# The first weight pieces of a mixer: split by ScalarE and VectorE into spare weight buffers, in a written order

## The chip, the cores and the metric

The kernel runs on one core of a Trainium2 chip, as one program. The metric is the device time of one launch in microseconds, the median of three runs. Engines are named as the profile names them: PE is TensorE, DVE VectorE, ACT ScalarE, POOL GpSimd, SP SyncE; PEld is PE's weight load.

## The reference, cut to what matters

Two layers run over 256 tokens of width 1024, in float32. Each layer has a mixer and a mixture of experts:

```
h = rms_norm(x) * (1 + scale_m(c)) + shift_m(c)
z = h @ w_in                       # 1024 x 7680, in one product
m = sum_i sigmoid(gate_i) * (attention_i(z) @ w_proj_i)      # i = A, B, C
x = x + gate_m(c) * (m @ w_out)
h = rms_norm(x) * (1 + scale_f(c)) + shift_f(c)
x = x + gate_f(c) * HierMoE(h)     # one group of four, two experts of eight in it
```

scale, shift and gate come from c by a product with ada_w. The change touches the beginning of `h @ w_in` in both layers.

## The kernel before

**The product with w_in.** It runs in 15 chunks of 512 columns, and a chunk in four pieces of 256 rows of w_in (128x1024 elements in SBUF). PE works in a float32 type of reduced precision, so every operand is kept as a high and a low part: for a piece of weights w, `whi` is a rounded copy (ACT, a CAST) and `wlo = w - whi` (DVE). The activations are treated the same way, as `hi` and `lo`, eight k-blocks of each. Three products are added up, hi·whi, hi·wlo and lo·whi, which makes 24 matmuls of 128x256 columns for a piece. `whi` and `wlo` come from the pool `wk` with two buffers each (tags w4a, w4b), so the CAST of a piece has to wait until PE has done all matmuls of the piece two before it. Pieces are called c0p0 to c0p3 for chunk 0, c1p0 to c1p3 for chunk 1, and so on.

**The beginning of a mixer.** `raw_t` transposes x into xT; the last of its four copies out of PSUM (`self.rest`, L272) is held back and issued by `modulated`. `modulated` works out rstd by some small instructions on DVE (L256, L233 to L242), PE spreads it over the partitions as R, and then, for each k, DVE multiplies xT by scale and R (L292), ACT adds the shift and writes hi (L294), and DVE writes lo (L289). In layer 0 scale and shift are finished only shortly before (L190, L195, L214). Ahead of that, the two pieces c0p0 and c0p1 are split: the CAST on ACT (L327), the subtraction on POOL (L330). c0p2 and c0p3 are split by `gemm` when the pool's two buffers come free, with the subtraction on DVE.

**Behind each chunk.** Where a chunk holds queries or keys, ACT copies four shifted strips out of PSUM (L484, four copies of 32x512), DVE multiplies by cosine and sine (L485, L486), and POOL adds (L487). In between DVE works on the next step's ada_w product (L175, with a first step on ACT, L173), which is needed much later.

**Order.** A scheduler with a timeline of its own orders the instructions of each engine. Only what `keep_in_program_order` names keeps its written order. Loads go over SP's queue into pairs of a pool of ten (`slot`, 2 MB for a pair); a load is issued when its pair is free.

The lines of the kernel after the change are a little shifted: split L327, L330 become L333, L334; L292, L289, L294 become L296, L290, L298; L484 to L487 become L487 to L490.

Of the kernel before, what the change touches and what calls it, by code (L numbers as in the profile page):

```python
# [10 lines left out]
F32 = mybir.dt.float32  # L11
F32R = mybir.dt.float32r
# [9 lines left out]
P = 128  # L22
SEQ = 256
D = 1024
KD = D // P
# [28 lines left out]
def bc(ap, at, n):  # L54

    a = [list(e) for e in ap.ap]
    a.insert(at, [0, n])
    return bass.AP(tensor=ap.tensor, offset=ap.offset, ap=a)


class Kernel:
# [197 lines left out]
    def raw_t(self, c):  # L259

        nc = self.nc
        p = self.acc()
        for kk in range(2):
            k = 2 * c + kk
            for t in range(2):
                nc.tensor.transpose(p[:, kk * 256 + t * P:kk * 256 + (t + 1) * P],
                                    self.x[:, t, k * P:(k + 1) * P], self.ident)
        to, p = self.xT[:, 2 * c:2 * c + 2, :], p.rearrange("p (k n) -> p k n", k=2)
        if c < 3:
            nc.scalar.copy(to, p)  # L270
        else:
            self.rest = lambda: self.tc.keep_in_program_order(nc.vector.tensor_copy(to, p))  # L272

    def hilo(self):
        return (self.wk.tile([P, KD, 256], F32R, name=nm, tag=tag) for nm, tag in (("hi", "w8a"), ("lo", "w8b")))

    def modulated(self, l):

        nc, xT = self.nc, self.xT
        hi, lo = self.hilo()  # L280
        scale, shift = self.mcol[l][:, 1, :], self.mcol[l][:, 0, :]
        r = self.rstd()
        self.rest()
        R = self.acc()[:, :256]
        for t in range(2):
            self.mm(R[:, t * P:(t + 1) * P], bc(r[:, t], 1, P), self.ident, t == 0, t == 1, skip_group_check=True)

        def low(k):
            nc.vector.scalar_tensor_tensor(lo[:, k, :], xT[:, k, :], shift[:, k:k + 1], hi[:, k, :].bitcast(F32),  # L289
                                           op0=OP.add, op1=OP.subtract)  # L290
        for k in range(KD):
            i = nc.vector.scalar_tensor_tensor(xT[:, k, :], xT[:, k, :], scale[:, k:k + 1], R,  # L292
                                               op0=OP.mult, op1=OP.mult)
            nc.scalar.activation(hi[:, k, :], xT[:, k, :], AF.Identity, bias=shift[:, k:k + 1])  # L294
            if k > 1:
                self.tc.keep_in_program_order(i)  # L296
            if k:
                low(k - 1)  # L298
        low(KD - 1)
        return hi, lo  # L300

    def to_hilo(self, src, done):

# [15 lines left out]
            two(k, p.rearrange("p (a n) -> p a n", a=2))  # L319
        return hi, lo  # L320

    def split(self, w, early=False):

        nc, n = self.nc, w.shape[1]
        whi, wlo = (self.wk.tile([P, n, 1024 // n], F32R, name=f"{nm}{n}", tag=tag, bufs=2)
                    for nm, tag in (("whi", "w4a"), ("wlo", "w4b")))
        c = nc.scalar.copy(whi, w)  # L327
        if early:
            self.tc.keep_in_program_order(c)
        (nc.gpsimd if early else nc.vector).tensor_sub(wlo, w, whi.bitcast(F32))  # L330
        return whi, wlo

    def gemm(self, pieces, hi, lo, prods):  # L333
# [44 lines left out]
    def mixer(self, l, fill):  # L378

        nc, tc, io = self.nc, self.tc, self.io  # L380
# [4 lines left out]
        def load(n):  # L385
            w = []
            for h in range(2):
                src = io["w_in"][l, n, h].rearrange("p (k n) -> p k n", k=4)
                w.append(self.slot().rearrange("p (k n) -> p k n", k=4))
                d = 2 if n == 0 else 4  # L390
                for k in range(0, 4, d):
                    nc.sync.dma_start(w[h][:, k:k + d], src[:, k:k + d])
            return w
        w0 = load(0)
# [26 lines left out]
        if l == 0:  # L421
# [4 lines left out]
                    self.square(t, half, self.x[:, t, hs], G[t][:, hs])  # L426
            for c in range(4):
                self.raw_t(c)
        halves = [self.split(w0[0][:, k:k + 2], True) for k in (0, 2)]
        hi, lo = self.modulated(l)  # L430

        def late_loads():
            if l == 0:
                self.small_loads(*(T0[:, o:o + 64 * a].rearrange("p (a n) -> p a n", a=a) for a, o in ((2, 1920), (4, 0))))
            nc.sync.dma_start(self.rwg, io["rw"][l])
            nc.sync.dma_start(self.cb, bass.AP(tensor=io["rb"].tensor, offset=l * NL, ap=[[0, P], [1, NL]]))
            nc.sync.dma_start(self.subg, bass.AP(tensor=io["subg"].tensor, offset=l * P, ap=[[0, P], [1, P]]))
            nc.sync.dma_start(bias, io["nab"][l])
            for t in range(2):
                nc.sync.dma_start(self.dmask[t], io["dmask"][:, t, :])  # L440

        def chunk(n):
            w = load(n) if n else w0
            if n == 0:
                nc.sync.dma_start(self.rope, io["rope"])
            if n == 4:
                late_loads()
            for _ in range(self.FILL[l][n]):
                if fill:
                    fill.pop(0)()  # L450
            evac, prods = [], []
            for kind, c0, wd, dst in SEGS[n]:
                if wd == 512:
                    z = [self.acc(), self.acc()]
                    prods += self.wide(z)
                    evac += [lambda t=t, z=z, kind=kind, dst=dst:
                             nc.scalar.copy(vdst[kind][:, t, dst:dst + 512], z[t]) for t in range(2)]
                    continue
                z = self.acc()
                if kind in vdst:  # L460
                    prods += [(z[:, t * 256:(t + 1) * 256], False, t, slice(c0, c0 + 256), t == 0) for t in range(2)]
                    evac.append(lambda z=z, kind=kind, dst=dst: nc.scalar.copy(
                        vdst[kind][:, :, dst:dst + 256], z.rearrange("p (t n) -> p t n", t=2)))
                    continue
                prods += self.flipped(z, c0)
                if kind == "g":
                    evac.append(lambda z=z, dst=dst: nc.scalar.activation(ga[dst // 2], z, AF.Tanh, scale=0.5))
                else:
                    evac.append(lambda z=z, kind=kind, dst=dst: place(z, kind, (qT2 if kind[1] == "q" else kT2)[dst]))
            pieces = [(k, w[k // 4][:, k % 4:k % 4 + 2]) for k in range(0, KD, 2)]  # L470
            if n == 0:
                pieces[:2] = [(*p, h) for p, h in zip(pieces, halves)]
            self.gemm(pieces, hi, lo, prods)
            self.pending += evac

        def place(z, kind, d):
            if kind[0] == "n":
                nc.scalar.mul(d, z, 0.125 if kind == "nq" else 1.0)
                return
            cos, sin = (bc(self.rope[:, i, :], 1, 2) for i in range(2))  # L480
            v = lambda a: a.rearrange("p (a n) -> p a n", a=2)
            sh = work("PD")
            for q in range(4):
                nc.scalar.copy(sh[32 * q:32 * q + 32], z[32 * (q ^ 1):32 * (q ^ 1) + 32])  # L484
            nc.vector.tensor_mul(v(d), v(z), cos)  # L485
            nc.vector.tensor_mul(v(sh), v(sh), sin)  # L486
            nc.gpsimd.tensor_add(d, d, sh)  # L487

        for n in range(9):
            chunk(n)  # L490
# [5 lines left out]
        for n in range(9, 15):  # L496
            chunk(n)
# [3 lines left out]
        hi, lo = self.to_hilo(tok, oT)  # L501
        srcs = [(0, 4), (4, 2), (6, 2)]
        for half in range(2):
            w = [self.slot().rearrange("p (k n) -> p k n", k=4) for _ in range(2)]
# [11 lines left out]
        hi, lo = self.to_hilo(None, [tok[i // 2][:, 512 * (i % 2):512 * (i % 2 + 1)].rearrange(  # L516
            "p (a n) -> p a n", a=2) for i in range(4)])
# [33 lines left out]
        for c in range(4):  # L551
            w = self.slot().rearrange("p (k n) -> p k n", k=KD)
# [3 lines left out]
            pieces = [(k, w[:, k:k + 4]) for k in (0, 4)]  # L556
# [8 lines left out]
            pieces = [(k, p, self.split(p)) for k, p in pieces]  # L565
# [563 lines left out]
```

## Time and profile before

| | |
|---|---|
| median of 3 runs | 1535.89 us (1535.77 to 1536.54) |
| the profiled execution | 1535.39 us, its span 1533.6 us |
| mean granted clock of PE | 0.911 |
| busy PE, DVE, ACT, POOL | 1228.9, 606.8, 384.7, 73.4 us |
| mixers | about 30 to 345 us and 777 to 1090 us |
| mixtures of experts | about 360 to 760 us and 1120 to 1520 us |

In the mixers PE is the busiest engine, in the mixtures of experts the DMA is. The mean over the span mixes the two, so what the change is worth has to be read in the mixers alone, at their beginning and at the pauses of PE in them. A row of a timeline gives the start, the duration, the engine, the line, the operation with its output and inputs, how many there are in a row, and in brackets the idle time of the engine before it with what ended that.

### The profile page before, as it was taken

Reading aid. Unit: us, or ns where it says so; the run is one execution under the profiler, and the core shown is the slowest. Engines: PE = TensorE matmul, PEld = TensorE weight load, DVE = VectorE, ACT = ScalarE, POOL = GpSimd, SP = SyncE. Lnnn points to the kernel's source line nnn. Section 1 sums busy time; section 2 is a strip of 40 time slices with the busy share of each in tenths; the row PEclk is TensorE's granted clock in tenths of the full one; section 3 lists DMA queues with packets and bytes.
Section 4 is the critical chain, followed back from the end, with each engine's and each line's share of the span. In section 5 each row is a group of like instructions: output and inputs, shape, how many; then the busy total and the mean of one; then the engine's idle time right before and its main releaser. Section 6 shows DMA issues by size and latency. Waiting matters only on the chain. (4 is left out here: it accounts for less than half of the span.)

```text
span 1533.6 us, 20114 instructions
## 1 busy us (share of the span) xinstructions
PE 1228.9 (80%) x8370; PEld 796.2 (52%) x8370; DVE 606.8 (40%) x1202; ACT 384.7 (25%) x681; POOL 73.4 (5%) x71
## 2 busy tenths in 40 slices
PE   5998999989777577677778899999897577577575
PEld 3888889874233133133257889899543133133132
DVE  2779884772112012011058797448322012011012
ACT  2656555450000000000046566544200000000001
POOL 1202000100000000000011110001000000000001
PEclk8999999999979889787889999999998788798898
DMA  9778683869999999999994874276899999999997
GB/s 369 284 296 319 275 326 146 343 246 403 428 425 427 427 427 427 427 426 428 421 372 172 340 312 186 110 315 235 318 425 426 427 426 427 427 426 427 426 427 294
DMA packets 52975, 543.93 MB, mean 355 GB/s; under 512 B 6784, under 2 KB 8336, under 8 KB 12048
## 3 DMA queue, kind: packets, MB, share of 16 engines
q1 hardware_dynamic: 52880, 542.60, 85.8%
q8 instruction: 68, 1.11, 0.3%
q14 instruction: 27, 0.22, 0.0%
HBM read 541.51 MB, written 1.06 MB: 354 GB/s over the span
## 5 line engine op out<-in xcount | busy, mean ns | idle before, releaser
L95 PE MATMUL acc<-rg,xg 128*32 128x512 f32 x2048 | 279.0, 687 | 116.3 <-DMA rg<-w 114.3
L95 PE MATMUL acc<-hi,wlo 128*128 128x256 f32 x896 | 260.0, 295 | 18.4 <-DVE wlo L330 18.0
L95 PE MATMUL acc<-lo,whi 128*128 128x256 f32 x896 | 253.4, 289 | 0.2 <-DVE lo L289 0.2
L95 PE MATMUL acc<-hi,whi 128*128 128x256 f32 x896 | 245.6, 290 | 6.5 <-ACT hi L294 4.9
L95 PE MATMUL acc<-rg,b 128*32 128x512 f32 (+1 forms) x1152 | 159.7, 688 | 93.7 <-DMA rg<-w2g 76.6
L95 PEld LDWEIGHTS acc<-rg,xg 128*32 128x32 f32 x2048 | 68.2, 118 | 303.7 <-issue 294.7
L330 DVE TENSOR_TENSOR wlo<-rg,whi 128x1024 fp32r<-128x1024 f32 x148 | 183.9, 1243 | 86.7 <-ACT whi L327 86.4
L327 ACT CAST whi<-rg 128x1024 fp32r<-128x1024 f32 x152 | 159.1, 1047 | 162.3 <-PE acc L95 136.1
L95 PEld LDWEIGHTS acc<-hi,wlo 128*128 128x128 f32 x896 | 175.1, 196 | 31.6 <-DVE wlo L330 24.2
L95 PEld LDWEIGHTS acc<-lo,whi 128*128 128x128 f32 x896 | 174.4, 196 | 1.6 <-DVE lo L289 0.5
L95 PEld LDWEIGHTS acc<-hi,whi 128*128 128x128 f32 x896 | 169.5, 196 | 10.5 <-ACT hi L294 5.5
L833 DVE TENSOR_TENSOR b<-b,acc 128x512 f32<-128x512 f32 x16 | 11.0, 687 | 350.5 <-PE acc L95 350.5
L95 PEld LDWEIGHTS acc<-rg,b 128*32 128x32 f32 x1152 | 35.5, 124 | 200.1 <-DMA rg<-w2g 112.6
L95 PEld LDWEIGHTS misc<-b,xn 128*128 128x128 f32 x512 | 124.6, 334 | 17.1 <-issue 15.7
L95 PE MATMUL misc<-b,xn 128*128 128x128 f32 x512 | 125.6, 404 | 4.1 <-DVEq L938 2.2
L832 ACT ACTIVATE b<-acc 128x512 f32<-128x512 f32 x16 | 9.6, 597 | 441.5 <-PE acc L95 441.5
L175 DVE SCALAR_TENSOR_TENSOR rg<-rg,sc 128x512 f32<-128x512 f32 x140 | 112.0, 832 | 4.4 <-DMA rg<-ada_w 2.5
L846 DVE TENSOR_TENSOR Y<-acc,grb 128x512 f32<-128x512 f32 x28 | 19.4, 692 | 235.5 <-PE acc L95 235.5
L826 ACT COPY b<-misc 128x256 f32<-128x256 f32 x16 | 6.0, 373 | 334.9 <-PE misc L825 334.9
L813 DVE TENSOR_SCALAR xg<-misc,mcol 128x128 f32<-128x128 f32 x128 | 44.3, 406 | 106.5 <-PE misc L95 106.5
L95 PE MATMUL acc<-wlo,hi 128*128 128x256 f32 (+1 forms) x256 | 79.8, 317 | 4.4 <-DVE wlo L330 4.3
L95 PE MATMUL acc<-whi,lo 128*128 128x256 f32 (+1 forms) x256 | 78.6, 314 | 1.5 <-DVE lo L310 1.3
(169 smaller groups left out, 1165.7 us busy)
## 6 DMA issues: line engine op xcount, KB each, us to landing
rg<-w SPq DMA_DIRECT2D x128, 2048.0 KB, 39.2
rg<-w2g SPq DMA_DIRECT2D x56, 2048.0 KB, 38.3
rg<-w_in SPq DMA_DIRECT2D x56, 1024.0 KB, 7.0
rg<-ada_w SPq DMA_DIRECT2D x48, 1024.0 KB, 8.5
rg<-w2c SPq DMA_DIRECT2D x12, 1024.0 KB, 29.6
rg<-w_proj SPq DMA_DIRECT2D x8, 1024.0 KB, 4.8
rg<-w_out SPq DMA_DIRECT2D x8, 1024.0 KB, 6.9
rg<-w_in SPq DMA_DIRECT2D x8, 512.0 KB, 15.4
```

Source lines behind the costliest of these rows:

```text
L95: return self.nc.tensor.matmul(out, lhsT, rhs, start=start, stop=stop, **kw)
L175: V.scalar_tensor_tensor(to, to, self.sc[:, k:k + 1], w[:, 0, cs] if j else self.ada_sum[:, cs], op0=OP.mult, op1=OP.add)
L327: c = nc.scalar.copy(whi, w)
L330: (nc.gpsimd if early else nc.vector).tensor_sub(wlo, w, whi.bitcast(F32))
L813: nc.vector.tensor_scalar(xg[:, k, :], p[:, kk * P:(kk + 1) * P], gf[:, k:k + 1], sf[:, k:k + 1], op0=OP.mult, op1=OP.add)
L826: nc.scalar.copy(ST, p[:, :256])
L832: nc.scalar.activation(a, h1, AF.Silu)
L833: nc.vector.tensor_mul(a, a, h3)
L846: nc.vector.tensor_mul(Y[:, hs], y[half], self.grb[:, hs])
```

## The change

The held-back copy of xT goes to ACT. `modulated` splits all four pieces of chunk 0 itself, one before every second k, with the CAST on ACT and the subtraction on DVE. The first two pieces go to a pair of the slots' pool, the other two to the pool `wk`. All these splits, and the multiplications of all eight k, keep their written order. `gemm` gets four finished pieces for chunk 0.

```diff
-            self.rest = lambda: self.tc.keep_in_program_order(nc.vector.tensor_copy(to, p))
+            self.rest = lambda: self.tc.keep_in_program_order(nc.scalar.copy(to, p))
...
-    def modulated(self, l):
+    def modulated(self, l, w):
...
+        parts = []
         for k in range(KD):
+            if k % 2 == 0:
+                parts.append(self.split(w[k // 2], self.slot("early") if k < 4 else None, self.tc.keep_in_program_order))
             i = nc.vector.scalar_tensor_tensor(xT[:, k, :], xT[:, k, :], scale[:, k:k + 1], R,
                                                op0=OP.mult, op1=OP.mult)
             nc.scalar.activation(hi[:, k, :], xT[:, k, :], AF.Identity, bias=shift[:, k:k + 1])
-            if k > 1:
-                self.tc.keep_in_program_order(i)
+            self.tc.keep_in_program_order(i)
             if k:
                 low(k - 1)
         low(KD - 1)
-        return hi, lo
+        return hi, lo, parts
...
-    def split(self, w, early=False):
+    def split(self, w, to=None, keep=lambda i: None):
 
         nc, n = self.nc, w.shape[1]
-        whi, wlo = (self.wk.tile([P, n, 1024 // n], F32R, name=f"{nm}{n}", tag=tag, bufs=2)
-                    for nm, tag in (("whi", "w4a"), ("wlo", "w4b")))
-        c = nc.scalar.copy(whi, w)
-        if early:
-            self.tc.keep_in_program_order(c)
-        (nc.gpsimd if early else nc.vector).tensor_sub(wlo, w, whi.bitcast(F32))
+        if to is None:
+            whi, wlo = (self.wk.tile([P, n, 1024 // n], F32R, name=f"{nm}{n}", tag=tag, bufs=2)
+                        for nm, tag in (("whi", "w4a"), ("wlo", "w4b")))
+        else:
+            whi, wlo = (to[:, i:i + 1024].rearrange("p (k n) -> p k n", k=n).bitcast(F32R) for i in (0, 1024))
+        keep(nc.scalar.copy(whi, w))
+        keep(nc.vector.tensor_sub(wlo, w, whi.bitcast(F32)))
         return whi, wlo
...
-        halves = [self.split(w0[0][:, k:k + 2], True) for k in (0, 2)]
-        hi, lo = self.modulated(l)
+        hi, lo, halves = self.modulated(l, [w0[k // 4][:, k % 4:k % 4 + 2] for k in range(0, KD, 2)])
...
-                pieces[:2] = [(*p, h) for p, h in zip(pieces, halves)]
+                pieces = [(*p, h) for p, h in zip(pieces, halves)]
```

What the scheduler makes of it is shown at three places of layer 1.

**ACT, the beginning of the mixer.** whi_5063, whi_5067, whi_5165, whi_5193 are c0p0 to c0p3 before, and whi_5226 and whi_5254 are c1p0 and c1p1. Before:

```order
L327 CAST whi_5063<-rg 128x1024
L327 CAST whi_5067<-rg 128x1024
L294 ACTIVATE hi<-rg,mcol_74 128x256 x7
L327 CAST whi_5165<-rg 128x1024
L294 ACTIVATE hi<-rg,mcol_74 128x256
L327 CAST whi_5193<-rg 128x1024
L327 CAST whi_5226<-rg 128x1024
L484 COPY rg<-acc 32x512 x4
L327 CAST whi_5254<-rg 128x1024
```

After, `rg<-rg` are c0p0 and c0p1, whi_5095 and whi_5105 are c0p2 and c0p3, and whi_5220 and whi_5248 are c1p0 and c1p1:

```order
L272 COPY rg<-acc 128x512
L333 CAST rg<-rg 128x1024
L298 ACTIVATE hi<-rg,mcol_74 128x256 x2
L333 CAST rg<-rg 128x1024
L298 ACTIVATE hi<-rg,mcol_74 128x256 x2
L333 CAST whi_5095<-rg 128x1024
L298 ACTIVATE hi<-rg,mcol_74 128x256 x2
L333 CAST whi_5105<-rg 128x1024
L333 CAST whi_5220<-rg 128x1024
L298 ACTIVATE hi<-rg,mcol_74 128x256 x2
L487 COPY rg<-acc 32x512 x4
L333 CAST whi_5248<-rg 128x1024
```

The last two hi (k 6 and 7) have moved behind the CAST of c1p0, which writes the buffer of c0p2.

**PE, from the last piece of chunk 0 to chunk 1.** Before, c0p3 (whi_5193, wlo_5194) is done before c1p0 (whi_5226) begins; the last rows of the one and the first of the other are:

```order
L95 MATMUL acc<-hi,wlo_5194 128x256
L95 MATMUL acc<-lo,whi_5193 128x256
L95 MATMUL acc<-hi,whi_5226 128x256 x2
L95 MATMUL acc<-hi,wlo_5227 128x256
L95 MATMUL acc<-lo,whi_5226 128x256
```

After, c0p3 (whi_5105, wlo_5106) begins behind two matmuls of c1p0 (whi_5220, wlo_5221). In the rows shown the first matmuls of both stand; behind them come the rest of c1p0 but one, then the other 20 matmuls of c0p3, and that one:

```order
L95 MATMUL acc<-lo,whi_5095 128x256
L95 MATMUL acc<-hi,whi_5220 128x256 x2
L95 MATMUL acc<-hi,whi_5105 128x256
L95 MATMUL acc<-hi,wlo_5106 128x256
L95 MATMUL acc<-hi,whi_5105 128x256
L95 MATMUL acc<-hi,wlo_5106 128x256
L95 MATMUL acc<-hi,wlo_5221 128x256
L95 MATMUL acc<-lo,whi_5220 128x256
```

The two pieces are mixed, and c0p3 ends one matmul before c1p0 does.

**DVE, from the end of chunk 0 to chunk 2.** wlo_5255, wlo_5283 and wlo_5325 are c1p1 to c1p3 before. Before:

```order
L330 TENSOR_TENSOR wlo_5255<-rg,whi_5254 128x1024
L485 TENSOR_TENSOR rg<-acc,rg 128x512
L486 TENSOR_TENSOR rg<-rg 128x512
L330 TENSOR_TENSOR wlo_5283<-rg,whi_5282 128x1024
L175 SCALAR_TENSOR_TENSOR rg<-rg,sc 128x512 x2
L330 TENSOR_TENSOR wlo_5325<-rg,whi_5324 128x1024
L175 SCALAR_TENSOR_TENSOR rg<-rg,sc 128x512 x3
L330 TENSOR_TENSOR wlo_5370<-rg,whi_5369 128x1024
```

After, wlo_5221 is c1p0 and wlo_5249, wlo_5277 and wlo_5319 are c1p1 to c1p3:

```order
L334 TENSOR_TENSOR wlo_5221<-rg,whi_5220 128x1024
L290 SCALAR_TENSOR_TENSOR lo<-rg,mcol_74,hi 128x256 x2
L488 TENSOR_TENSOR rg<-acc,rg 128x512
L489 TENSOR_TENSOR rg<-rg 128x512
L334 TENSOR_TENSOR wlo_5249<-rg,whi_5248 128x1024
L334 TENSOR_TENSOR wlo_5277<-rg,whi_5276 128x1024
L488 TENSOR_TENSOR rg<-acc,rg 128x512
L489 TENSOR_TENSOR rg<-rg 128x512
L175 SCALAR_TENSOR_TENSOR rg<-rg,sc 128x512 x6
L334 TENSOR_TENSOR wlo_5319<-rg,whi_5318 128x1024
L334 TENSOR_TENSOR wlo_5364<-rg,whi_5363 128x1024
```

The split of c1p0 has moved ahead of the last two lo, and six L175 in a row now stand ahead of c1p3's split. A run of six before stood at chunk 6, ahead of c6p1, and is gone there.

## Rows read from the trace of the kernel before

**Rows 1.** Windows: busy time by engine, granted clock, DMA share, GB/s.

```profile
792.00:1090.00 298.00, 278.45 (x2101) 254.50 (x2104) 214.10 (x399) 164.10 (x280) 28.03 (x14) 0.98 0.62 243
1120.00:1520.00 400.00, 284.56 (x1746) 117.61 (x1741) 60.39 (x130) 12.72 (x29) 2.88 (x4) 0.87 1.00 425
```

**Rows 2.** PE's waits, windows 46 to 345, 64 to 140 and 816 to 880.

```profile
PE acc L95 <- DVE wlo L330: 11.2, 11, 3.5
...
PE acc L95 <- DVE wlo L330: 7.0, 5, 3.5
...
PE acc L95 <- DVE wlo L330: 8.1, 8, 3.4
```

**Rows 3.** Timeline of DVE, beginning of layer 1's mixer.

```profile
779.60 2.35 DVE L239 SCALAR_TENSOR_TENSOR rsq<-rsq 128x2 f32<-128x2 f32 x1
781.98 2.26 DVE L240 TENSOR_TENSOR rsq<-rsq 128x2 f32<-128x2 f32 x1
784.28 0.16 DVE L241 TENSOR_TENSOR rsq<-rsq 128x2 f32<-128x2 f32 x1
```

**Rows 4.** Timeline of POOL, beginning of layer 1's mixer.

```profile
779.59 4.64 POOL L330 TENSOR_TENSOR wlo<-rg,whi 128x1024 fp32r<-128x1024 f32 x2 [0.66 <-ACT whi L327]
```

**Rows 5.** Timeline of PE, layer 1, chunks 0 and 1.

```profile
787.09 0.58 PE L95 MATMUL acc<-hi,whi 128*128 128x256 f32 x1 [1.11 <-ACT hi L294]
...
797.82 0.40 PE L95 MATMUL acc<-hi,whi 128*128 128x256 f32 x2
...
800.70 0.40 PE L95 MATMUL acc<-hi,whi 128*128 128x256 f32 x2
...
805.04 0.39 PE L95 MATMUL acc<-hi,wlo 128*128 128x256 f32 x1 [0.88 <-DVE wlo L330]
...
811.99 0.39 PE L95 MATMUL acc<-hi,wlo 128*128 128x256 f32 x1 [0.36 <-DVE wlo L330]
```

**Rows 6.** Timeline of ACT, layer 1, end of chunk 0.

```profile
798.02 1.05 ACT L327 CAST whi<-rg 128x1024 fp32r<-128x1024 f32 x1 [1.79 <-PE acc L95]
800.18 2.34 ACT L484 COPY rg<-acc 32x512 f32<-32x512 f32 x4 [1.11 <-PE acc L95]
802.55 1.05 ACT L327 CAST whi<-rg 128x1024 fp32r<-128x1024 f32 x1
```

**Rows 7.** Timeline of DVE, layer 1, chunk 1.

```profile
803.77 1.22 DVE L330 TENSOR_TENSOR wlo<-rg,whi 128x1024 fp32r<-128x1024 f32 x1
...
808.34 2.45 DVE L175 SCALAR_TENSOR_TENSOR rg<-rg,sc 128x512 f32<-128x512 f32 x2
...
811.86 2.07 DVE L175 SCALAR_TENSOR_TENSOR rg<-rg,sc 128x512 f32<-128x512 f32 x3
```

**Rows 8.** Timeline of DVE, beginning of layer 0's mixer.

```profile
30.95 0.17 DVE L195 TENSOR_TENSOR mcol<-adap,acol 128x8 f32<-128x8 f32 x1 [0.67 <-PE adap L193]
31.15 2.31 DVE L214 SCALAR_TENSOR_TENSOR mcol<-mcol,gcol 128x8 f32<-128x8 f32 x1
```

**Rows 9.** Timeline of PE, layer 0, chunks 0 to 2.

```profile
34.66 0.58 PE L95 MATMUL acc<-hi,whi 128*128 128x256 f32 x1 [3.75 <-ACT hi L294]
...
46.45 0.40 PE L95 MATMUL acc<-hi,whi 128*128 128x256 f32 x2
...
53.67 0.39 PE L95 MATMUL acc<-hi,wlo 128*128 128x256 f32 x1 [0.88 <-DVE wlo L330]
...
64.01 0.63 PE L95 MATMUL acc<-whi,hi 128*128 128x512 f32 x2
```

**Rows 10.** Timeline of PE, the longest wait for wlo but two.

```profile
824.85 0.50 PE L95 MATMUL acc<-wlo,hi 128*128 128x512 f32 x1 [1.50 <-DVE wlo L330]
```

**Rows 11.** Windows behind the three longest waits (3.5, 1.5 and 3.4 us).

```profile
137.80:143.07 5.27, 5.27 (x24) 5.27 (x25) 5.27 (x7) 0.17 (x1) 2.79 (x1) 0.50 0.73 300
824.85:830.00 5.15, 5.15 (x23) 4.25 (x24) 5.15 (x10) 1.55 (x2) 0.00 (x0) 1.00 0.94 387
877.18:880.58 3.40, 3.40 (x16) 3.40 (x17) 3.40 (x4) 0.00 (x0) 2.11 (x1) 0.52 0.24 99
```

## The prediction

> **What bounds the kernel now.** I read first the windows over a mixer and over a mixture of experts [rows 1]. In the mixer PE is busy 278 of 298 us and the DMA 0.62; in the mixture of experts the DMA share is 1.00 at 425 GB/s. So a mixer ends when PE is through, and as the experts' stream behind it runs at the DMA's pace whenever it starts, I take each microsecond won or lost in a mixer to reach the end unchanged. Then I read what PE waits for in the mixers [rows 2]: nearly all is `wlo` from DVE, in layer 0 11.2 us, the longest 3.5, and in layer 1 8.1 in chunks 2 to 6 alone, the longest 3.4. Last, the timelines of the two beginnings. In layer 1, L239 and L240, on two numbers per partition, take 2.35 and 2.26 us where their neighbour L241 takes 0.16 [rows 3], and they end as POOL's two subtractions do, 4.64 us from 779.59 [rows 4]. PE gets its first matmul of the mixer at 787.09 [rows 5]. In layer 0, L214, on 128x8 numbers, takes 2.31 us in the same way [rows 8].
>
> **What the change takes away.** POOL's splits, in both layers. Layer 1: L239 and L240 at 0.16 each give 2.35 + 2.26 - 0.32 = 4.29 us. DVE gets c0p0's subtraction instead (1.22, [rows 7]), between L242 and the first multiplication. There it lies beside PE's making of R, in place of the copy L272 that goes to ACT; so I cost it at nothing, and at up to 1.2 if that cover fails. PE starts at 782.80, and c0p3 could start at T = 797.82 - 4.29 = 793.53 [rows 5]. The moved splits of c0p1 to c0p3 lie between the multiplications while PE works on the piece before; a pair of k costs DVE some 2.8 us of PE's 2.88 for a piece at full clock (24 matmuls from 797.82 to 800.70, so 0.12 each) and of more at half clock, where PE still is at the start. I count nothing for them.
> Layer 0: L214 at 0.16 gives 2.15. But c0p0's subtraction now stands ahead of L195, and its operand is late, since c0's weights land just then: its CAST cannot end much before the 30.95 at which L195 started, and 1.25 of the gain goes. PE starts at 34.66 - 0.9 = 33.76 [rows 9]. From there to c0p3 I take layer 1's 10.73 us (before 11.79 here, with a stall for lo that POOL caused); T = 44.49 against 46.45, 1.96 earlier.
>
> **What it adds: the end of chunk 0.** The last two hi and lo stand behind the split of c1p0 on ACT and DVE, and that split writes c0p2's buffers, so it begins only when PE is through with c0p2, at T. The CAST started 0.2 after that before too (798.02 against 797.82, [rows 5, 6]), and from a CAST's start to the first hi·wlo of its piece takes 805.04 - 802.55 = 2.49. So PE's first hi·wlo of c1p0 comes at T + 2.69, and ahead of it PE has six matmuls of 0.12: 2 us lost. Then 42 matmuls follow, and c1p0 ends at T + 7.7 in place of T + 5.8.
> The mixing costs more than that. c0p3 ends one matmul ahead of c1p0, and both c1p1's buffer and the four strips of chunk 0 (L487) wait for it. Before, the strips began 0.52 ahead of the end of chunk 0 and took until 802.55, 2.37 us [rows 6], under the cover of c1p0. Now nothing covers them: they start at T + 7.1, c1p1's CAST at T + 9.46, its first hi·wlo at T + 11.95. Before, that was 805.04 - 797.82 = 7.22 behind c0p3's start. Lost in layer 1: 4.7.
> In layer 0 DVE has L488, L489 and one L175 ahead of c1p1's subtraction: T + 9.46 + 1.2 + 0.7 + 1.22 gives a first hi·wlo at T + 12.6; before 53.67 - 46.45 = 7.22 as well; lost 5.4. Of the pauses that followed in chunk 1 none is left in the new order, so chunk 1 ends 22 + 48 matmuls later, at T + 21.0, against 64.01 - 46.45 = 17.56 before: 3.4 lost.
> **The clock.** Before c1p1 PE now stands still for nearly 3 us, does two matmuls, and waits 1 to 2 us more. [...]
> **The six L175.** In layer 1 they now stand ahead of c1p3's split. The strips of chunk 0's second half end at about T + 13.8 on ACT, L488 and L489 at T + 15.0. The six take 0.69 each (2.07 for three, [rows 7]), 4.1, and POOL's rotary add beside them stretches two of them, as in 2.45 for two: 1.1 more. With 1.2 for the subtraction the first hi·wlo comes at T + 21.4; before 811.99 - 797.82 = 14.17 [rows 5]. So the loss since T is 7.2 by then, including the 4.7, and 2.9 net of the 4.29.
> The rows first: two L175 beside POOL's add took 2.45, two of the three without it 1.38; and L239 and L240 lasted as long as POOL's two subtractions [rows 3, 4, 7]. [...]
>
> **Later chunks.** DVE has 2.88 - 1.22, some 1.7 us, to spare between two splits; what the order puts there beyond that makes PE wait. I summed the excess over the order's rows (L175 0.69, L485 with L486 1.2). Layer 1, c2 to c6: 8.1 before (the waits have 8.1 too, [rows 2], so the count holds), 5.6 after, as the run ahead of c6p1 is gone: -2.5, and -1.7 for the half clock behind it [rows 11]. Behind chunk 6 -0.6. Layer 0, c2 to c7: 9.5 before, of which 7.0 showed as waits [rows 2]; 11.4 after, in the same proportion 8.4: +1.4. The pause of 3.5 is replaced by two of about 2.3 and 1.5: half of its 2.6 given back, -1.3 (bounds 0 and 2.6). Behind chunk 7 the count goes from 19 to 16, but waits there and in chunk 1 together were only 11.2 - 7.0 = 4.2, since attention's matmuls cover them: -0.3.
> **The lost pair** of the slots delays a load of chunk 2 or of ada_w until PE has done c0p1, some 9 us behind its start. Chunk 2 begins when the other two pieces and chunk 1 are through, six pieces of 2.88 or 17 us later, and 2 MB at 425 GB/s take 5: nothing.
>
> **Sum.** Layer 0: -1.96 + 3.4 + 2.2 + 1.4 - 1.3 - 0.3 = +3.4. Layer 1: -4.29 + 7.2 - 4.2 - 0.6 = -1.9. Together +1.5. The profiled execution's 1535.39 (span 1533.6 and 1.8 around it) lies 0.5 below the median; on the median it gives 1537.4. That is +0.1%, and within 0.2%, 3.1 us either way, is what a measurement of this kernel cannot tell from no change: 1532.8 to 1539.0.
>
> **Rivals.**
> *The clock decides (slower).* It halves behind each pause over 2 us: at the start of chunk 1 in layer 0 (in the sum), at chunk 7 (nothing given back, +1.3), and in layer 1 again ahead of c1p3 (+1.7). 1537.4 + 3.0 = 1540.4. It decides from the pause length, between 1.50 and 3.37, where the clock goes; the rows leave that open. Chance 0.33.
> *The starts' gain passes on (faster).* The clock stays up through the new pauses (-2.2), layer 0's later runs stay hidden behind attention's matmuls (-1.4), and the half clock of chunk 7 goes whole (-1.3): 1532.5. For it: of the late runs little showed. Against it: of those in c2 to c7, 7.0 of 9.5 did. Chance 0.17.
> *The change does not free DVE.* If L239, L240 and L214 are slow for another reason than POOL, 4.3 and 2.2 come back: 1543.9. The ends that fall together speak against it: 0.04.
> The forecast, within 0.2%: 0.46. The sum's own range, with the clock between its bounds in layer 0, is 1535 to 1539.
>
> **Range.** From the faster rival, 1532.0, to the slower one and a little above, 1541.0; beyond it I leave 0.1 above and 0.08 below. Faster by over 0.2%: 0.16 (the faster rival, mostly). Slower: 0.36 (the clock's rival nearly whole, the last one). Within: 0.48.
>
> **What would show it.** L239 and L240 at 0.16, and from L239 of layer 1 to PE's first hi·whi about 3.2 us in place of 787.09 - 779.60 = 7.5; in layer 0 the first hi·whi at about 33.8. At the end of chunk 0 a pause of some 2 us in parts, then one of nearly 3 us ended by ACT and 1 to 2 more ended by wlo, in both layers. In layer 1 a wait ahead of c1p3 ended by wlo behind six L175, and none of 3.4 ahead of c6p1. Chunk 1 ends 3 to 4 us later in layer 0, and about 3 later in layer 1. What would make it wrong: a CAST of c1p0 that does not hold hi up; a clock that stays up; runs in layer 0 that show more or less than in proportion.

## The result, and the profile after

The changed kernel takes 1546.85 us (1544.14 to 1550.12, six runs), the kernel before 1535.61 in the same comparison (1532.39 to 1536.54). The ratio is 1.0079 [1.0066, 1.0092]: slower by 0.8%, some 11 us. The forecast was 1537.4, the range up to 1541.0. The first profiled execution is the slowest of the six, with a span of 1548.3 us against 1533.6; a second profile of the same kernel (below) has 1545.0, with a time of 1546.79 us, close to the median.

First comes the beginning of layer 1's mixer after the change, which answers to [rows 3]. This is the timeline of DVE:

```profile
792.46 0.16 DVE L239 SCALAR_TENSOR_TENSOR rsq<-rsq 128x2 f32<-128x2 f32 x1
792.66 0.16 DVE L240 TENSOR_TENSOR rsq<-rsq 128x2 f32<-128x2 f32 x1
```

Both are short now. From L239 to the first hi·whi of PE it was 7.49 us before [rows 3, 5], and it is 795.57 - 792.46 = 3.11. The timeline of PE, after, over chunks 0 to 2 of layer 1 (answers to [rows 5]; L334 is wlo, L333 whi):

```profile
795.57 1.22 PE L95 MATMUL acc<-hi,rg 128*128 128x256 f32 x4 [1.53 <-ACT hi L298]
...
808.06 0.80 PE L95 MATMUL acc<-hi,whi 128*128 128x256 f32 x3 [1.18 <-ACT whi L333]
817.27 0.50 PE L95 MATMUL acc<-hi,whi 128*128 128x256 f32 x2 [2.67 <-ACT whi L333]
818.66 0.58 PE L95 MATMUL acc<-hi,wlo 128*128 128x256 f32 x1 [0.89 <-DVE wlo L334]
828.24 0.46 PE L95 MATMUL acc<-hi,wlo 128*128 128x256 f32 x1 [2.30 <-DVE wlo L334]
...
835.43 0.73 PE L95 MATMUL acc<-whi,hi 128*128 128x512 f32 x2
837.45 1.13 PE L95 MATMUL misc<-rg 64*128 64x256 f32 x8 [1.29 <-POOL rg L490]
```

PE now pauses at three places in a row: for the CAST of c1p0 (808.06), for the CAST of c1p1 and then its wlo (817.27, 818.66), and for c1p3's wlo (828.24). The kernel before paused there only for c1p1's wlo, 0.88 us, and for c1p3's, 0.36 [rows 5]. What holds the CAST of c1p1 stands on ACT, whose timeline answers to [rows 6]: the four strips are now uncovered, and the CAST comes right behind them.

```profile
813.80 2.34 ACT L487 COPY rg<-acc 32x512 f32<-32x512 f32 x4 [4.98 <-PE acc L95]
816.17 1.05 ACT L333 CAST whi<-rg 128x1024 fp32r<-128x1024 f32 x1
```

Layer 0 begins with the same pauses, for the CAST of c1p0 (45.05) and for the CAST and the wlo of c1p1 (54.26, 57.38). The timeline of PE (answers to [rows 9]):

```profile
33.51 1.22 PE L95 MATMUL acc<-hi,rg 128*128 128x256 f32 x4 [1.96 <-ACT hi L298]
45.05 0.80 PE L95 MATMUL acc<-hi,whi 128*128 128x256 f32 x3 [1.18 <-ACT whi L333]
54.26 0.79 PE L95 MATMUL acc<-hi,whi 128*128 128x256 f32 x2 [2.67 <-ACT whi L333]
57.38 0.58 PE L95 MATMUL acc<-hi,wlo 128*128 128x256 f32 x1 [2.33 <-DVE wlo L334]
...
70.15 0.73 PE L95 MATMUL acc<-whi,hi 128*128 128x512 f32 x2
74.51 2.08 PE L95 MATMUL misc<-rg 64*128 64x256 f32 x8 [3.63 <-POOL rg L490]
76.52 0.79 PE L95 MATMUL acc<-wlo,hi 128*128 128x512 f32 x1
```

The eight matmuls on `misc` read what POOL's rotary add has written, and PE waits 3.63 us for that add. In the kernel before the same matmuls did not wait. Rows of its PE, in chunk 2 of layer 0:

```profile
68.35 0.50 PE L95 MATMUL acc<-wlo,hi 128*128 128x512 f32 x1 [0.64 <-DVE wlo L330]
...
70.54 0.39 PE L95 MATMUL acc<-whi,lo 128*128 128x512 f32 x1
70.86 1.13 PE L95 MATMUL misc<-rg 64*128 64x256 f32 x8
```

PE's order has changed as well. Before, the eight stand behind all twelve matmuls of c2p1, the last ten of which begin at 68.35. After, in both layers, they stand behind the first two of c2p1 (70.15 and 835.43), and the other ten come behind them (from 76.52 in layer 0).

The timeline of DVE shows an L175 that waited for ada_w ahead of the multiplications for the rotary (L488, L489), in layer 0 and in layer 1:

```profile
68.93 1.41 DVE L175 SCALAR_TENSOR_TENSOR rg<-rg,sc 128x512 f32<-128x512 f32 x2 [2.11 <-DMA rg<-ada_w]
70.26 0.68 DVE L488 TENSOR_TENSOR rg<-acc,rg 128x512 f32<-128x512 f32 x1
...
821.94 5.10 DVE L175 SCALAR_TENSOR_TENSOR rg<-rg,sc 128x512 f32<-128x512 f32 x6
826.97 2.35 DVE L334 TENSOR_TENSOR wlo<-rg,whi 128x1024 fp32r<-128x1024 f32 x2
833.05 0.75 DVE L175 SCALAR_TENSOR_TENSOR rg<-rg,sc 128x512 f32<-128x512 f32 x1 [3.73 <-DMA rg<-ada_w]
834.33 0.69 DVE L488 TENSOR_TENSOR rg<-acc,rg 128x512 f32<-128x512 f32 x1 [0.52 <-ACT rg L487]
```

L488 also needs the strips from ACT:

```profile
66.67 2.35 ACT L487 COPY rg<-acc 32x512 f32<-32x512 f32 x4 [1.11 <-PE acc L95]
...
831.94 2.35 ACT L487 COPY rg<-acc 32x512 f32<-32x512 f32 x4 [5.16 <-PE acc L95]
```

In layer 0 the strips are done at 69.02 and L488 begins at 70.26, so the L175 hold it up by 1.2 us. In layer 1 the strips end at 834.29, behind the L175, and L488 begins at 834.33: there the L175's wait of 3.73 us holds up nothing.

SP's timeline dates the load of ada_w in layer 1. It was issued at 828.21, when c1p3's split (826.97, the first of the two) had read its weights and so freed their pair:

```profile
828.21 0.80 SPq L159 DMA_DIRECT2D rg<-ada_w  x2
```

The clock comes on top. These are windows of the changed kernel behind two pauses of layer 0, at the last attention of layer 0, and behind c1p3's pause in layer 1 (busy times by engine, then granted clock). They answer to [rows 11]:

```profile
54.00:61.00 7.00, 4.42 (x21) 4.13 (x22) 6.73 (x10) 3.66 (x7) 1.99 (x2) 0.54 0.64 262
...
74.51:80.00 5.49, 5.49 (x16) 3.99 (x17) 5.49 (x7) 0.00 (x0) 1.65 (x1) 0.50 0.45 190
282.00:293.00 11.00, 8.80 (x49) 6.47 (x48) 3.30 (x8) 3.17 (x9) 0.00 (x0) 0.53 0.61 226
828.24:832.00 3.76, 3.76 (x19) 3.76 (x20) 1.08 (x1) 0.06 (x1) 0.00 (x0) 0.55 0.69 246
```

The same split of the weights is done by the same kind of instruction in both kernels, so its starts on DVE, piece by piece, date how far the changed kernel lags. In layer 0 it is +7.0 at c3p0 (77.95 before, 84.97 after) and +12.7 at the mixer's last pieces. In layer 1 it is +7.0 at c0p2 (793.39, 800.41), +16.3 at c1p3 (810.72, 826.97), +18.9 at c3p0, +16.1 at c7p0 and +14.5 at the end. So layer 0 lost 12.7 us and layer 1 only 1.8, and the mixtures of experts between and behind them hardly changed it. In the second profile it is 10.9 and 1.3.

The largest single step of the lag lies at layer 0's last attention, from +7.7 to +12.9. Two splits there, before and then after:

```profile
273.75 1.22 DVE L330 TENSOR_TENSOR wlo<-rg,whi 128x1024 fp32r<-128x1024 f32 x1
284.65 1.22 DVE L330 TENSOR_TENSOR wlo<-rg,whi 128x1024 fp32r<-128x1024 f32 x1 [2.30 <-ACT whi L327]
```

```profile
281.48 1.22 DVE L334 TENSOR_TENSOR wlo<-rg,whi 128x1024 fp32r<-128x1024 f32 x1
297.54 1.22 DVE L334 TENSOR_TENSOR wlo<-rg,whi 128x1024 fp32r<-128x1024 f32 x1 [2.31 <-ACT whi L333]
```

### The profile page after: what moved, and what is told of

Its sections match the earlier page's. It is cut to its first block, busy times and chain, and to the rows that moved or that the text cites. A ratio compares the mean times of both kernels' runs of the same rounds, so it can differ in the third digit from the quotient of the medians.

```text
span 1548.3 us, 20121 instructions
## 1 busy us (share of the span) xinstructions
PE 1242.5 (80%) x8370; PEld 801.2 (52%) x8370; DVE 604.3 (39%) x1204; ACT 384.8 (25%) x683; POOL 61.0 (4%) x67
## 5 line engine op out<-in xcount | busy, mean ns | idle before, releaser
L95 PE MATMUL acc<-hi,wlo 128*128 128x256 f32 x864 | 249.1, 292 | 14.2 <-DVE wlo L334 13.7
L95 PE MATMUL acc<-hi,whi 128*128 128x256 f32 x864 | 236.8, 289 | 11.0 <-ACT whi L333 9.3
L95 PE MATMUL acc<-lo,whi 128*128 128x256 f32 x864 | 243.2, 287 | 0.0
L334 DVE TENSOR_TENSOR wlo<-rg,whi 128x1024 fp32r<-128x1024 f32 x148 | 186.8, 1263 | 82.6 <-ACT whi L333 82.3
L333 ACT CAST whi<-rg 128x1024 fp32r<-128x1024 f32 x148 | 154.8, 1048 | 158.4 <-PE acc L95 147.2
L95 PEld LDWEIGHTS acc<-hi,wlo 128*128 128x128 f32 x864 | 167.6, 194 | 26.1 <-DVE wlo L334 19.2
L95 PEld LDWEIGHTS acc<-hi,whi 128*128 128x128 f32 x864 | 161.9, 194 | 17.0 <-ACT whi L333 11.7
L95 PEld LDWEIGHTS acc<-lo,whi 128*128 128x128 f32 x864 | 167.1, 194 | 1.7 <-issue 1.0
L95 PEld LDWEIGHTS misc<-b,xn 128*128 128x128 f32 x512 | 124.6, 334 | 17.5 <-issue 16.1
L175 DVE SCALAR_TENSOR_TENSOR rg<-rg,sc 128x512 f32<-128x512 f32 x140 | 109.7, 818 | 12.1 <-DMA rg<-ada_w 8.4
## 6 DMA issues: line engine op xcount, KB each, us to landing
rg<-w_in SPq DMA_DIRECT2D x8, 512.0 KB, 16.1
```

The source lines that it names most:

```text
L95: return self.nc.tensor.matmul(out, lhsT, rhs, start=start, stop=stop, **kw)
L175: V.scalar_tensor_tensor(to, to, self.sc[:, k:k + 1], w[:, 0, cs] if j else self.ada_sum[:, cs], op0=OP.mult, op1=OP.add)
L333: keep(nc.scalar.copy(whi, w))
L334: keep(nc.vector.tensor_sub(wlo, w, whi.bitcast(F32)))
```

## The experiments

Theory A: the order at the end of chunk 0, with the last hi and lo behind the split of c1p0, costs the time, with what follows from it. Theory B: the lost pair of the slots makes ada_w late. Theory C: DVE is too full for the additional subtractions, or the run of L175 is the whole cost.

**Split behind hi.** The changed kernel with one dependence of order more (the mark is set in `modulated`):

```diff
+        self.mark = [h, low(KD - 1)]
...
-            whi, wlo = done[0] if done else self.split(w)
+            whi, wlo = done[0] if done else self.split(w, keep=self.behind)
...
+    def behind(self, i):
+        if self.mark:
+            self.tc.add_manual_dep(i.ins, self.mark.pop(0).ins.name, mybir.DependencyInfo(
+                mybir.DependencyClass.NoSync, mybir.DependencyReason.DATA), reason="behind")
```

> The changed kernel, but the split of the first piece of chunk 1 is held behind the last hi (ACT) and the last lo (DVE); the pair of the slots, the splits on DVE and the written order stay. Theory A (that order alone costs the time: mixed pieces, uncovered strips, the run of six L175 and the late ada_w follow from it): some 1529 us, the two beginnings' gains of 2.7 and 3.8 us stay and the 11 are gone. Theory B (the lost pair of the slots makes ada_w late, which stops DVE at chunk 2): the waits for ada_w stay, some 1538 us. Theory C (DVE has no room for the four subtractions): no better than 1544 us.

Measured: 1535.15 us, ratio to the kernel before 1.0005 [0.9996, 1.0014]. The 11 us are back, with the pair of the slots, the splits on DVE and their order unchanged, so A holds against B and C as far as the sign goes. The dependence also changes what the scheduler deals out behind it: the eight matmuls on `misc` are back behind the whole of c2p1 in both layers, without a wait. But the beginnings' gain did not show in the time: layer 1 keeps it (the lag goes from +4.9 at the end of layer 0 to +0.5 at its own), layer 0 loses it again. About half of that loss, 3.6 us from c1p1 to c2p0, arises in layer 0's chunk 1. Of this kernel first a row of DVE's timeline, then one of PE's, then the window behind it:

```profile
54.20 2.52 DVE L175 SCALAR_TENSOR_TENSOR rg<-rg,sc 128x512 f32<-128x512 f32 x2
```

```profile
58.10 0.58 PE L95 MATMUL acc<-hi,wlo 128*128 128x256 f32 x1 [2.49 <-DVE wlo L335]
```

```profile
58.10:64.60 6.50, 6.50 (x32) 6.50 (x33) 4.19 (x8) 1.04 (x1) 0.00 (x0) 0.53 0.50 180
```

The scheduler has put two L175 ahead of c1p2's split, where the kernel before had them behind it; beside POOL's add they take 2.52 us (the two at 68.93 in the changed kernel, with POOL idle, took 1.41), PE pauses 2.49, and the granted clock is 0.53 over the 6.5 us behind it.

**DVE alone.** The kernel before, with the early subtraction on DVE and nothing else:

```diff
-        (nc.gpsimd if early else nc.vector).tensor_sub(wlo, w, whi.bitcast(F32))
+        nc.vector.tensor_sub(wlo, w, whi.bitcast(F32))
```

> The kernel before, but the two early subtractions go from POOL to DVE; nothing else. Theory A: no hi is displaced, so L239 and L240 shrink to 0.16 us, one subtraction of 1.2 us lies open on DVE, layer 1's first hi.whi comes some 3 us earlier, layer 0's about as before: 1532 us. Theory C: DVE is too full at the beginning, 1536 us or more. Theory B says nothing of it (no pair is taken).

Measured: 1541.5 us, 1.004 [1.0026, 1.0053]. This is a miss for A's number, and it is C's number (1536 or more), but not C's mechanism: at c1p0 layer 0 is 0.5 us ahead, and layer 1 gains some 3.4 us up to there, so DVE has room at the beginning. L239 and L240 are short, but without a written order the two subtractions land ahead of L239 and ahead of L240 and delay rstd. Layer 0 loses 10 us behind its chunk 0, by an order dealt out anew: pauses for wlo of 2.66 and 2.14 us in chunks 1 and 2, with the clock at 0.66 behind the first over 3.3 us and at 0.54 behind the second over 3.5.

**Pair alone.** The kernel before, with the two early splits in a pair of the slots, POOL kept:

```diff
+        if early:
+            to = self.slot("early")
+            whi, wlo = (to[:, i:i + 1024].rearrange("p (k n) -> p k n", k=n).bitcast(F32R) for i in (0, 1024))
+        else:
...
```

> The kernel before, but the two early splits go into a pair of the slots, still with POOL's subtraction; the other two pieces of chunk 0 then find the pool's buffers free. Theory A: no hi stands behind a split of chunk 1, the stretched L239 and L240 stay: 1535 to 1537 us. Theory B (the lost pair): ada_w late and DVE stopped at chunk 2, 1540 us or more.

Measured: 1544.98 us, 1.007 [1.0057, 1.0083], which is B's number but not B's mechanism. The longest wait of an L175 for ada_w is 1.5 us there, where the kernel before has 1.4 and the changed one 3.7, so no late load stops DVE. With POOL's subtractions kept, L239 is at 2.36 us again, as a row of DVE's timeline shows, and PE's timeline has a pause of 2.38 us in chunk 1 of layer 0:

```profile
788.46 2.36 DVE L239 SCALAR_TENSOR_TENSOR rsq<-rsq 128x2 f32<-128x2 f32 x1
```

```profile
61.10 0.39 PE L95 MATMUL acc<-hi,wlo 128*128 128x256 f32 x1 [2.38 <-DVE wlo L334]
```

Its largest single loss, 5.1 us, is at layer 0's last attention, as in the changed kernel. This run also limits what the first one shows: no piece is mixed here, since c1p0's split (49.05) begins behind the last lo (43.55 to 44.63), and yet the kernel is 10.7 us slower. An order dealt out anew can cost as much without any mixing.

**Ada later.** The changed kernel, with the ada_w products dealt to later chunks:

```diff
-    FILL = (0, 1, 0, 3, 0, 2, 2, 3, 2, 2, 3, 2, 3, 0, 1), (0, 0, 2, 2, 2, 2, 2, 2, 1, 3, 0, 0, 0, 0, 0)
+    FILL = (0, 0, 0, 4, 0, 2, 2, 3, 2, 2, 3, 2, 3, 0, 1), (0, 0, 0, 3, 3, 2, 2, 2, 1, 3, 0, 0, 0, 0, 0)
```

> The changed kernel, but the ada_w products are dealt out to later chunks (layer 0: none in chunk 1, four in chunk 3; layer 1: none in chunk 2, three each in chunks 3 and 4). The mixed pieces at the end of chunk 0 stay, no six L175 stand ahead of the last piece of chunk 1, and no L175 of chunk 1 or 2 can wait for ada_w. Theory A with its chain: the loss at the end of chunk 0 stays (4.7 and 6 us with the clock), the 8 us at chunks 1 to 2 go: some 1539 us. Theory B: as A for the wait, 1539 us. Theory C': the run of L175 is the whole cost: 1533 us.

Measured: 1547.31 us, 1.0083 [1.007, 1.0096], as slow as the changed kernel. In its profile the end of chunk 0 costs nearly what it did: in layer 0 there are pauses of 1.18, 2.66 and 1.09 us, where the changed kernel has 1.18, 2.67 and 2.33, with no L175 ahead of c1p1's or c1p3's split, so that cost is the mixing's own. No L175 waits more than 1.1 us for ada_w any more, but at c3p0 of layer 0 the lag is 5.8 us where it was 7.0, not the 4 less of the expectation, and at the end of layer 0 it is 11.1. The eight matmuls on `misc` stand behind the first two of c2p1 here too, and PE waits for POOL's add as before:

```profile
74.12 1.14 PE L95 MATMUL misc<-rg 64*128 64x256 f32 x8 [2.71 <-POOL rg L490]
...
834.59 2.08 PE L95 MATMUL misc<-rg 64*128 64x256 f32 x8 [3.83 <-POOL rg L490]
```

The waits for ada_w are thus no separate cost that could simply be taken off.

**L175 behind the split.** The first experiment, and in layer 0 the ada_w product of chunk 1 issued behind c1p2's split:

```diff
-            for _ in range(self.FILL[l][n]):
-                if fill:
-                    fill.pop(0)()
+            held = [fill.pop(0) for _ in range(self.FILL[l][n]) if fill]
+            if l or n != 1:
+                for f in held:
+                    f()
...
             self.gemm(pieces, hi, lo, prods)
+            if l == 0 and n == 1:
+                with self.tc.issue_after(self.wlos[-2].ins):
+                    for f in held:
+                        f()
```

> As the run with the split behind hi, and besides, in layer 0, the ada_w product of chunk 1 (L175) is held behind the split of c1p2. If the moved L175 are what ate the gain there (in that run two L175 beside POOL's add stood ahead of c1p2's split, a pause of 2.49 us and then 7 us at half clock): about 5.9 us less, some 1529 us, below both kernels. Rival: the excess of DVE's work only moves to the next split, 1534 to 1537 us.

Measured: 1532.27 us median, but 0.9999 [0.9987, 1.0012] in the comparison of runs, and its twelve runs spread from 1529.65 to 1538.93. The mechanism is seen in the profile (span 1530.4): the pause of 2.49 is one of 1.03, the clock is 1.00 from 37 to 111 us, and at c2p0 of layer 0 the lag is -1.5 where it was +1.8. The gain of the time cannot be called shown here.

**Strips behind the CAST.** The changed kernel with its mixed pieces; the strips of chunk 0 wait, in order, for the CAST of c1p1:

```diff
             for q in range(4):
-                nc.scalar.copy(sh[32 * q:32 * q + 32], z[32 * (q ^ 1):32 * (q ^ 1) + 32])
+                i = nc.scalar.copy(sh[32 * q:32 * q + 32], z[32 * (q ^ 1):32 * (q ^ 1) + 32])
+                if q == 0 and self.first:
+                    self.first = self.behind(i)
...
```

> The changed kernel with its mixed pieces, but the four strips of chunk 0 are held behind the CAST of c1p1 in both layers. By the prediction's step (the strips, 2.37 us, uncovered ahead of that CAST): c1p1's first hi.wlo comes at T + 10.3 in place of 11.95, 1.7 us less in layer 1, as much or more in layer 0 (L488, L489 and the L175 no longer stand ahead of its subtraction), and less of the clock: 1540 to 1543 us. Rival (the displaced hi and the waiting buffer alone do it): the same as the changed kernel, 1546 to 1548 us.

Measured: 1554.19 us, 1.0133 [1.0118, 1.0148]. The number is a miss, the local term is right: from c1p0's to c1p1's split layer 1 loses 2.95 us (+3.22 to +6.17) in place of 4.67 (+8.94 to +13.61), so the strips are 1.7 of that loss. Layer 0 ends at +6.9 in place of +12.7. But the scheduler dealt layer 1's L175 out anew, and layer 1 loses 11.2 us in place of 1.8. Of this kernel a row of DVE's timeline and one of PE's behind it:

```profile
825.97 2.74 DVE L175 SCALAR_TENSOR_TENSOR rg<-rg,sc 128x512 f32<-128x512 f32 x4 [1.74 <-DMA rg<-ada_w]
```

```profile
831.10 0.79 PE L95 MATMUL acc<-wlo,hi 128*128 128x512 f32 x1 [3.53 <-DVE wlo L335]
```

**The changed kernel again,** with no edit, for a second profile.

> The changed kernel once more, unchanged, for a second profile. If the half clock at layer 0's last attention (282 to 293 us, 5.2 us lost against before) comes from the order of its instructions, it is there again; if from the one execution, it is gone and the span is some 5 us shorter.

Measured: 1546.79 us in a single run, span 1545.0. The half clock at layer 0's last attention is there again, a window of 11 us at 0.53:

```profile
280.00:291.00 11.00, 8.80 (x49) 6.28 (x47) 3.37 (x8) 3.22 (x8) 0.00 (x0) 0.53 0.63 235
```

So it comes with this order and not with the one execution: the lag goes from +5.8 to +11.0 there, as from +7.7 to +12.9 in the first profile. Of the 3.3 us between the two spans 1.9 have arisen by chunk 10 of layer 0, 1.4 of them in chunks 8 and 9; the rest was not traced.

**The copy alone.** The kernel before, with the last copy of xT on ACT (`nc.scalar.copy` in `raw_t`).

> The kernel before, with only the last copy of xT on ACT. All theories: it was 0.69 us of DVE in a gap ahead of the first multiplication, no change by itself, 1534 to 1536 us, unless the scheduler deals the L175 out anew as in the other runs; then 2 to 8 us more.

Measured: 1534.12 us, 0.9999 [0.999, 1.0008], and no split more than 0.2 us from its place. This part of the change is worth nothing by itself.

**Layer 0 alone.** The first experiment, with the dependence left out in layer 1 (`if l: self.mark = []`).

> The changed kernel with the split of c1p0 held behind the last hi and lo in layer 0 alone. If the two layers' losses are separate and add up as read from the profiles (layer 0 with the split held ends 4.9 us later than before, layer 1 as changed adds some 1.5), 1540 to 1542 us, about midway between the changed kernel and the one with both held. If one layer carries the whole loss, 1535 or 1546 us.

Measured: 1538.55 us, 1.0036 [1.0024, 1.0048]. Layer 0 ends at +3.8, and layer 1 goes through its mixed end of chunk 0 and comes out at +2.95, 0.8 less than it began with. So most of the 11 us is layer 0's; layer 1, with its mixed pieces, gives back most of what its beginning gains (with the split held in both layers it gained 4.4).

**Spread.** The kernel of "L175 behind the split", with the ada_w products dealt more evenly:

```diff
-    FILL = (0, 1, 0, 3, 0, 2, 2, 3, 2, 2, 3, 2, 3, 0, 1), (0, 0, 2, 2, 2, 2, 2, 2, 1, 3, 0, 0, 0, 0, 0)
+    FILL = (0, 1, 1, 2, 0, 2, 2, 2, 1, 3, 3, 2, 3, 0, 2), (0, 0, 2, 1, 2, 2, 2, 2, 2, 3, 0, 0, 0, 0, 0)
```

> As the run with the split held and L175 behind c1p2's split, and the ada_w products dealt out to the chunks more evenly (layer 0: one in chunks 1, two in 3, and so on; layer 1 one fewer in chunk 3), so that the order has less DVE work between two splits beyond what one piece of PE covers: 6.9 us in chunks 1 to 8 of layer 0 in place of 13.1 before, 8.4 in layer 1 in place of 11.6. If the excess of L175 between splits is what is left of the loss: 1525 to 1529 us, below both kernels. Rival (the covers of the later chunks move it elsewhere): 1531 to 1535 us.

Measured: 1528.87 us (1525.85 to 1531.99), 0.9967 [0.9955, 0.9978]: 0.3% faster than the kernel before, 1.2% faster than the changed one, and in the range of the expectation. The profiled run is the fastest of its eight. The mean granted clock in the two mixers, the number behind the busy times, says where part of it lies; in the kernel before it was 0.96 in both (28 to 345 and 776 to 1095 us). Windows of this kernel, and then of the changed one:

```profile
28.00:345.00 317.00, 291.01 (x2189) 260.07 (x2193) 241.97 (x460) 173.39 (x296) 26.70 (x15) 0.97 0.73 284
775.00:1085.00 310.00, 287.62 (x2154) 259.51 (x2158) 224.09 (x427) 171.85 (x294) 27.18 (x15) 0.98 0.65 254
```

```profile
28.00:357.00 329.00, 298.56 (x2165) 267.01 (x2169) 243.19 (x459) 173.03 (x296) 26.35 (x15) 0.93 0.70 272
780.00:1110.00 330.00, 300.68 (x2239) 267.13 (x2243) 228.06 (x435) 175.10 (x305) 27.40 (x15) 0.96 0.64 252
```

**The dealing alone.** The kernel before with that FILL.

> The kernel before with the same dealing out of the ada_w products as in the run before this one and nothing else: tells how much of that run's time the dealing alone gives. Its order has 8.4 us of excess in chunks 1 to 8 of layer 0 (13.1 before), 11.5 in layer 1 (11.6): 1530 to 1533 us if the excess counts, 1534 to 1536 if not.

Measured: 1537.57 us, 1.0018 [1.0009, 1.0028]. Its range is missed. Up to layer 0's last attention it was some 5 us ahead, which fits an excess that is 4.7 us smaller; there the clock was 0.51 over 14 us, and it lost 7.9. A window of that stretch:

```profile
269.00:283.00 14.00, 12.35 (x57) 9.19 (x58) 4.35 (x10) 4.25 (x11) 0.00 (x0) 0.51 0.45 164
```

Layer 1 gains 6.9 us in the run before and loses 0.3 here. So the gain of the run before is not the dealing's alone; it needs the changed beginning as well.

## Why the prediction was wrong

The steps up to the end of chunk 1 were right, most of them to a few tenths; the largest miss among them is 1.1 us. Measured in the first profile after:

| step | predicted | measured |
|---|---|---|
| layer 1, from L239 to the first hi·whi | 3.2 | 3.11 |
| layer 1, c1p1's first hi·wlo behind T | 11.95 | 818.66 - 806.72 = 11.94 |
| layer 1, c1p3's first hi·wlo behind T | 21.4 | 828.24 - 806.72 = 21.5 |
| layer 0, first hi·whi | 33.76 | 33.51 |
| layer 0, c1p1's first hi·wlo behind T | 12.6 | 57.38 - 43.71 = 13.7 |
| layer 0, end of chunk 1 against before | -1.96 + 3.4 + 2.2 = +3.6 | 67.19 - 64.01 = +3.2 |

(T is the end of c0p2 on PE: its last matmul starts at 806.60 and at 43.59 and takes 0.12.) That POOL's splits stretched L239 and L240 was borne out too: with these splits gone both are at 0.16 (0.15 in the run with DVE alone), and with them kept, in the run with the pair alone, L239 is at 2.36; and two L175 beside POOL's add take 2.52 again, in the split-behind-hi run. The clock did halve behind the pause at c1p1, as forecast for layer 0 (0.54 in 54.00 to 61.00), and in layer 1 too (0.56 in 818.66 to 822.00). The 2.2 us that the sum has for it in layer 0, with bounds of 0 and 2.6, was the author's estimate, and no run shows it by itself: behind that pause PE worked at 0.58 from 57.38 to 61.00 in the first profile and at 0.50 from 58 to 62 in the second, which at the clock of 1.00 that came next would have taken some 1.5 and 2.0 us less (estimated from these windows).

What failed is the step "Later chunks". It summed DVE's excess between two splits, so the only wait of PE that it counted was the one for wlo, and at attention it counted a gain. The sum is short by 13 us in the first profile and by 10.6 in the second.

First, chunk 2. PE's order had moved there as well, and I had not read it: the eight matmuls on `misc` stand behind two matmuls of c2p1 in place of twelve, so PE comes to them ten matmuls of 0.23 us earlier and waits for POOL's add, 3.63 us in layer 0 and 1.29 in layer 1. Over all runs this place and the wait go together. In chunk 2 of every layer of every run where the eight stand there PE waits for the add, 1.29 to 3.83 us, and in none where they stand behind the whole piece. I had also costed the L175 by their durations alone, and none of them by what it waits for. The load of ada_w is issued when c1p3's split is done (828.21 behind 826.97), and the run of six that I had put ahead of that split delays the load as well. But of these waits little reached PE: 1.2 of the 3.63 us in layer 0 and nothing in layer 1. In layer 1 the wait for the add is 1.29 us as well in the runs with DVE alone, with the pair alone and with the dealing spread, where no L175 of chunk 2 waits for ada_w; and with the ada_w products dealt later PE waits 2.71 and 3.83 us. The forecast on the lost pair of the slots ("nothing") stands, since the run with the pair alone has no long wait for ada_w.

From c2p0 to c3p0 layer 0 lags 3.9 us more (2.4 in the second profile), with a clock of 0.50 behind that wait (74.51 to 80.00). From c1p3 to c3p0 layer 1 lags 2.6 more, and a clock of 0.55 behind c1p3's pause (828.24 to 832.00) is part of it: the sum had left that out and the slower rival had it, at 1.7. The prediction had nothing for either in layer 1, and 1.4 for all of c2 to c7 in layer 0.

Second, the last attention of layer 0, where nothing was forecast: +5.2 us, in a stretch of 11 us at a clock of 0.53, in both profiles of the changed kernel.

Third, the rest of layer 0 came out about as the sum had it, but by luck. From c3p0 to the first piece behind chunk 14 (269.07 before) layer 0 lost 0.7 us, and gained 0.8 in the second profile, where the sum had it flat. In between it lost 4.9 (5.1) up to c7p0 and got 4.2 (5.9) back behind it. The term -1.3 for the half clock at chunk 7 (half of 2.6, estimated from the 5.27 us at 0.50 in [rows 11]) is not settled: the first profile has two stretches at 0.50 in its place (135.5 to 138.9 and 166.2 to 169.6), the second has a clock of 1.00 from 80 to 280 us.

What was right behind chunk 1 is layer 1's return, in kind if not in size: -2.8 from c3p0 to c7p0, of it -3.5 from c6p0 to c6p1, as the run of six before c6p1 is gone, where the forecast was -4.2 for c2 to c6; and -1.6 behind c7p0, forecast -0.6.

The sum by layers: layer 0 +12.7 for +3.4, layer 1 +1.8 for -1.9. The slower rival had the right sign and a mechanism that took part; its 1540.4 was too little, as beside chunk 1 of layer 0 it had half clocks at chunk 7 and c1p3 only.

What is shown by removal: with the split of c1p0 held behind the last hi and lo the 11 us are gone (1535.15), and with that in layer 0 alone most of them (1538.55). So the order that follows from the end of chunk 0 carries the loss. How much of it is the mixing itself and how much the work that the scheduler then deals differently was not separated in the time: the profiles give 4.7 us in layer 1 and 6.4 in layer 0 up to c1p1's first hi·wlo, but the pair alone loses 10.7 without a mixed piece. Why the clock falls at layer 0's last attention is open.

## What to carry to other kernels

When a list scheduler fills an engine's idle time, an edit at the beginning of a phase moves filler in all of it: read the new order past the edit, on every engine, PE's own too, and cost each moved instruction by what it waits for and which buffer it frees, beside its duration. Before a wait is called a cost, look whether what stands behind it could have begun any earlier. A split into a double buffer that was put ahead of work on the current piece turned two pieces that overlapped into two that waited for each other (here pauses of 1.18 and 2.67 us in each layer); a dependence of order alone gave 11 us back. To judge an edit at one place, hold the filler still or deal it anew for both kernels, as the last two runs did (1528.87 and 1537.57 us, the former with one ada_w product of layer 0 held as well).

## What was not expected of the hardware

No one length of pause decided the clock. In the pair's run a pause of 2.38 us (at 61.10, after two matmuls and 0.39 us more) was followed by a clock of 1.00; in the split-behind-hi run 2.49 gave 0.53, and in the DVE run 2.14 gave 0.54. And at layer 0's last attention the clock fell to 0.53 (282.00 to 293.00) behind no pause over 0.79 us: in the first profile after, PE was busy 5.21 of 6 us just before, and 5.21 of 6 at the same place of the kernel before, where the clock stayed at 1.00. A window of the changed kernel, and then two of the kernel before, the second behind the place:

```profile
276.00:282.00 6.00, 5.21 (x39) 4.53 (x38) 3.62 (x7) 5.49 (x10) 0.00 (x0) 1.00 0.28 115
```

```profile
268.00:274.00 6.00, 5.21 (x41) 4.62 (x40) 3.31 (x7) 4.89 (x8) 0.00 (x0) 1.00 0.41 172
274.00:284.00 10.00, 9.22 (x82) 7.91 (x83) 4.77 (x10) 5.20 (x12) 0.00 (x0) 1.00 0.79 311
```

What told the two apart is left open. Behind the place both kernels have the same order; ahead of it they differ, for example in 28 matmuls of 128x128 on `misc` that the kernel before has in one row (from 262.57) and the changed one in two groups (8 from 269.05, 20 from 272.93).
